# PSUM banks of the expert stage handed out in the order they come back, and the scatter sums and the next gather placed later

## The chip, the cores and the metric

The kernel runs on one core of a Trainium2 chip. The metric is the device time of one execution in microseconds, as the median of the runs shown. One execution was also taken by the hardware profiler; its trace is what the rows below come from. The engines are named as the profile names them: PE (matmul; PEld is its weight load), DVE (vector), ACT (scalar), POOL and SP (the queue that issues the weight loads).

## The reference, cut to what matters

The program is a two-layer transformer block followed by a second block. What the change touches is the mixture of experts: 256 tokens, 8 experts, two of them for each token.

```
for e in range(8):
    y = (silu(h @ w_gate[e]) * (h @ w_up[e])) @ w_down[e]     # 1024 -> 3584 -> 1024
    out = out + gates[..., e:e+1] * y
```

All weights are 4-byte floats: three matrices of 1024 x 3584 for each expert, some 352 MB in all for this stage, which takes about half of the time.

## The kernel before, in words

**Units.** The expert stage reads its weights in units of 1 MB (a tile of 128 x 2048). An expert has 42 of them, and the program passes them in one fixed order written out in Python. The expert's 3584 columns are cut into four slices f (1024, 1024, 1024, 512). For a slice come its gate units, its up units, and then the down units of the slice before it (`STEPS`, `wide`, `down`). A slice of 1024 has 4 + 4 + 4 units, so the first slice of a later expert has 4 gate units, 4 up units and the 2 last down units of the expert before it; slices 1 and 2 have twelve units each, and slice 3 has eight. Below, f0 to f3 are these slices and "unit 5 of f1" counts from the slice's first gate unit.

**One unit.** Each weight tile is split into two parts so that fp32 products can be made from faster matmuls. ACT casts it to `w_hi` (line 86), DVE subtracts to get `w_lo` (line 87), PE multiplies. There are three pairs of `w_hi`/`w_lo`, so ACT's cast for unit n + 3 waits until PE has finished unit n. `Weights.ahead` issues the split of unit n + 2 before the other work of unit n, so on ACT and DVE, which work in program order, everything placed in unit n stands behind the split of unit n + 2. SP issues the load into a freed raw buffer (line 148).

**Two kinds of experts.** Only the tokens of an expert are computed, gathered into 128 columns. If an expert has at most 64 tokens, both parts of the tokens fit side by side into one stationary operand and a unit takes 8 matmuls of 512 columns (line 1306, `few_`); otherwise it takes 12 (lines 1297, 1299, 1301, `many`). PE chooses at run time. By the lines that run, experts 0, 1, 2, 4 and 7 are of the small kind here and 3, 5 and 6 of the large kind.

**Work beside the units.** `later(n, do)` puts a piece of work n units ahead, and `later(n, do, 1)` puts it behind the matmuls of that unit. Each 512-column result of a gate or an up lies in a PSUM bank: one unit after the result is complete ACT copies it out (line 1374), one unit after that PE turns it into another bank (lines 1359, 1363), and one unit after that ACT (silu, line 1383) or DVE (product, line 1391) reads it. When an expert's last down unit is done, its two accumulators are split (lines 443, 444), and `scatter` sends the result back to the token order: for each half c of the columns and each half t of the tokens two matmuls (line 1439) into a bank, and one unit later DVE adds the bank, times the gate, into `x` (line 1447). The two sums of c = 0 are made after unit 3 of the next expert's f1, those of c = 1 after unit 4. `gather` prepares the following expert: DVE builds a selection matrix (lines 1185 and 1187), PE multiplies it twice into a bank (line 1323), each result is split by ACT and DVE (lines 443, 444), and a transpose follows (lines 1331, 1333). It starts at unit 7 of f1, its matmuls come after units 8, 10 and 12.

**Banks.** Two of the eight PSUM banks hold the accumulators `acc`. The other six form the pool `psum`, whose tiles the framework hands out with the waits that the reuse of a tile's bank needs. `wide` asks for its two banks before its first unit.

Of the kernel before, what the change touches and what calls it, by code (L numbers as in the profile page):

```python
# [203 lines left out]
def lm_kernel(ctx: ExitStack, tc: tile.TileContext, g, out: bass.AP, start=None, stop=None):  # L204
# [244 lines left out]
    class Prep:  # L449
# [67 lines left out]
        def spread(self, psum, tag="ps"):  # L517

            ps = psum.tile([128, 512], F32, name=tag)
            nc.tensor.matmul(ps[:, 0:T], ones, flat(self.diag), start=True, stop=True)  # L520
            R = work.tile([128, T], F32, name="R", bufs=2)
            nc.scalar.copy(R, ps[:, 0:T])  # L522
            self.R = R
            return R[:, None, :].to_broadcast([128, 2, T])

# [604 lines left out]
    def moe(prep, stack):  # L1130
# [83 lines left out]
        psum = pool_of(stack, "moe_ps", 6, True)  # L1214
# [34 lines left out]
        def experts(W, r0, picked=None, late=None):  # L1249
# [61 lines left out]
            def gather(e):  # L1311
                P = picked if picked is not None and e == 0 else pick(e, r0)
                X[e] = parted(xp, 8, "xe", bufs=2)
                if not r0:
                    more[e] = nc.values_load(counts[0:1, e:e + 1], engines=[mybir.EngineType.PE], min_val=0, max_val=T)
                yield
                for half_ in range(2):
                    hs = slice(half_ * 4, half_ * 4 + 4)
                    ps = psum.tile([128, 4, CAP], F32, name="ps")
# [6 lines left out]
                    split_psum(sl(X[e][1:], S_, hs), ps)  # L1326
                    yield
                PT[e] = p.tile([128, T], F32R, name="PT", bufs=2)
                ps = psum.tile([128, 512], F32, name="ps")
# [3 lines left out]
                nc.scalar.copy(PT[e], ps[:, 0:T])  # L1333

# [5 lines left out]
            def wide(name, e, f, after={}):  # L1340

                nh, n = SIZES[f] // 512, 2048 // SIZES[f]
                ps = [psum.tile([128, 512], F32, name="ps") for _ in range(nh)]
                for u in range(8 // n):
                    step(name, lambda w: products(
                        e, [(ps[c], sl(X[e], S_, u * n + k), sl(w, S_, k, half(c))) for k in range(n) for c in range(nh)],
                        lambda i: u == 0 and i < nh, lambda i: u == 8 // n - 1 and i >= (n - 1) * nh))
                    if u in after:
                        after[u]()
                return ps  # L1350

            def turn(e, s):

                ps = psum.tile([128, 4, 128], F32, name="ps")
# [11 lines left out]
                return ps  # L1366

            def turn_later(e, c, ps, use):
# [3 lines left out]
                def copy():  # L1372
                    box["s"] = xp.tile([128, 512], F32, name="s", bufs=2)
                    nc.scalar.copy(box["s"], ps)  # L1374

                later(1 + c, copy)
                later(2 + c, lambda: box.update(ps=turn(e, box["s"])), 1)
                later(3 + c, lambda: use(box["ps"]))
# [19 lines left out]
            def down(e, f):  # L1398
# [9 lines left out]
                if not last or e < LAST:  # L1408
# [8 lines left out]
                    if last:  # L1417
                        for c in range(2):
                            later(1 + c, lambda a=sl(y, S_, half(c)), b=acc[c]: split_psum(a, b))
                            scatter(e, c, 3 + c)  # L1420
# [13 lines left out]
            def scatter(e, c, n=None):  # L1434

                def multiply(t):
                    ps = psum.tile([128, 512], F32, name="ps")
# [7 lines left out]
                def add(t, ps):  # L1445
                    xs = x[:, t, half(c)]
                    nc.vector.scalar_tensor_tensor(xs, ps, gates[:, t, e:e + 1], xs, op0=OP.mult, op1=OP.add)

                for t in range(2):
                    if n is None:  # L1450
                        multiply(t)
                    else:
                        later(n, lambda t=t: multiply(t), 1)
# [9 lines left out]
            for s in STEPS + [None]:  # L1463
# [5 lines left out]
                if f == 1 and e < LAST:  # L1469
                    gather_later(STEPS[STEPS.index((e, NS - 1)) + 1][0], 7)  # L1470
# [819 lines left out]
```

## Time and profile before

| what | value |
|---|---|
| runs shown (3) | median 1785.62 us, 1784.87 to 1785.79 us |
| profiled execution, its own time | 1785.14 us |
| its span in the trace | 1783.4 us |
| mean granted PE clock | 0.985 |
| expert stage in the trace | from about 434 us (unit 0 split) to about 1390 us |
| weight loads of the stage | 336 of 1 MB |

In the windows below, each stretch of the expert stage runs from DVE's split of a slice's first unit to that of the next slice's first unit, so it holds one slice's split work. "Busy" of PE is the time in which matmuls are in flight, which isn't the same as PE at its peak. A timeline row gives the start, the duration (of several merged instructions together), and in brackets how long the engine had been idle and what ended that.

### The profile page before, as it was taken

How to read it: one execution, taken by the hardware profiler on the slowest of the kernel's cores; microseconds unless marked ns; L12 is line 12 of the kernel's file. 1: busy time of each engine (PE TensorE's matmuls, PEld its weight loads, DVE VectorE, ACT ScalarE, POOL GpSimd, SP SyncE). 2: the span in 40 equal slices, each digit the busy share in tenths (PEclk: the TensorE clock that was granted, in tenths of full speed). 3: DMA queues.
4: the chain of work that ended last, by engine and by line, in shares of the span. 5: the costliest groups of instructions: out<-in, count | busy, mean ns of one | idle time of the engine just before them, and what ended most of it. 6: DMA issues, size and time to landing. Idle time of an engine off the chain costs nothing. (4 is left out here: it accounts for less than half of the span.)

```text
span 1783.4 us, 24452 instructions
## 1 busy us (share of the span) xinstructions
PE 1707.3 (96%) x9381; PEld 1438.6 (81%) x9381; DVE 1428.9 (80%) x1365; ACT 1157.1 (65%) x1103; POOL 57.5 (3%) x104
## 2 busy tenths in 40 slices
PE   8999999999999898999999999999999899999999
PEld 7879999998777776778877778888777678789998
DVE  4666655775999999898899998887899788579776
ACT  4544444464888788887787876776879544546553
POOL 1001000120000000000000000000001100000000
PEclk9999999999999999999999999999999899999999
DMA  7546555448999999999899998998997443236552
GB/s 253 165 130 203 189 189 187 159 146 308 375 373 412 353 399 410 367 412 347 314 390 353 401 396 308 349 352 314 345 387 285 148 153 128 77 112 200 188 189 71
DMA packets 176043, 483.18 MB, mean 271 GB/s; under 512 B 8183, under 2 KB 71793, under 8 KB 161554
## 3 DMA queue, kind: packets, MB, share of 16 engines
q1 hardware_dynamic: 173762, 476.09, 72.8%
q0 software_dynamic: 2128, 4.91, 1.0%
q8 instruction: 113, 1.85, 0.4%
q14 instruction: 40, 0.33, 0.1%
HBM read 479.92 MB, written 1.05 MB: 270 GB/s over the span
## 5 line engine op out<-in xcount | busy, mean ns | idle before, releaser
L87 DVE TENSOR_TENSOR w_lo<-raw,w_hi 128x2048 fp32r<-128x2048 f32 x219 | 499.8, 2290 | 135.7 <-ACT w_hi L86 135.5
L86 ACT CAST w_hi<-raw 128x2048 fp32r<-128x2048 f32 x219 | 417.1, 1909 | 225.3 <-issue 87.2
L411 PE MATMUL ps<-hT_hi,w_hi 128*128 128x256 f32 x704 | 199.6, 284 | 0.1
L412 PE MATMUL ps<-hT_lo,w_hi 128*128 128x256 f32 x704 | 199.5, 283 | 0.1
L413 PE MATMUL ps<-hT_hi,w_lo 128*128 128x256 f32 x704 | 199.3, 283 | 0.0
L87 DVE TENSOR_TENSOR w_lo<-ahead,w_hi 128x2048 fp32r<-128x2048 f32 x78 | 177.0, 2287 | 20.7 <-ACT w_hi L86 20.6
L87 DVE TENSOR_TENSOR w_lo<-spare,w_hi 128x2048 fp32r<-128x2048 f32 x75 | 170.2, 2287 | 21.3 <-ACT w_hi L86 21.2
L1306 PE MATMUL ps<-w_lo,xe 128*128 128x512 f32 x560 | 162.6, 413 | 19.6 <-DVE w_lo L87 18.3
L1306 PE MATMUL ps<-w_hi,xe 128*128 128x512 f32 x560 | 162.6, 412 | 17.6 <-ACT s L1374 8.4
L86 ACT CAST w_hi<-ahead 128x2048 fp32r<-128x2048 f32 x78 | 147.6, 1906 | 33.9 <-PE ps L1299 12.3
L86 ACT CAST w_hi<-spare 128x2048 fp32r<-128x2048 f32 x75 | 141.9, 1907 | 29.8 <-PE ps L1299 8.7
L1306 PEld LDWEIGHTS ps<-w_lo,xe 128*128 128x128 f32 x560 | 103.3, 192 | 64.3 <-DVE w_lo L87 43.2
L1306 PEld LDWEIGHTS ps<-w_hi,xe 128*128 128x128 f32 x560 | 104.2, 194 | 42.5 <-ACT s L1374 10.1
L412 PEld LDWEIGHTS ps<-hT_lo,w_hi 128*128 128x128 f32 x704 | 134.6, 191 | 1.5 <-DVE hT_lo L444 0.8
L411 PEld LDWEIGHTS ps<-hT_hi,w_hi 128*128 128x128 f32 x704 | 134.6, 191 | 1.0 <-ACT R L522 0.2
L413 PEld LDWEIGHTS ps<-hT_hi,w_lo 128*128 128x128 f32 x704 | 134.6, 191 | 0.3 <-DVE w_lo L87 0.3
L87 DVE TENSOR_TENSOR w_lo<-hT_lo,w_hi 128x2048 fp32r<-128x2048 f32 (+1 forms) x53 | 118.9, 2245 | 14.5 <-ACT w_hi L86 14.3
L86 ACT CAST w_hi<-hT_lo 128x2048 fp32r<-128x2048 f32 (+1 forms) x53 | 99.5, 1880 | 22.3 <-PE acc L1299 7.7
L1297 PE MATMUL ps<-w_hi,xe 128*128 128x512 f32 x336 | 95.3, 405 | 2.0 <-ACT s L1374 2.0
L1301 PE MATMUL ps<-w_lo,xe 128*128 128x512 f32 x336 | 92.4, 397 | 0.0
L1299 PE MATMUL ps<-w_hi,xe 128*128 128x512 f32 x336 | 92.3, 396 | 0.0
L1306 PE MATMUL acc<-w_lo,hp 128*128 128x512 f32 x280 | 90.2, 405 | 1.9 <-DVE w_lo L87 1.0
(480 smaller groups left out, 3393.1 us busy)
## 6 DMA issues: line engine op xcount, KB each, us to landing
raw<-in_moe_w_up_dram SPq DMA_DIRECT2D x38, 1024.0 KB, 7.6
raw<-in_moe_w_gate_dram SPq DMA_DIRECT2D x34, 1024.0 KB, 8.0
raw<-in_moe_w_down_dram SPq DMA_DIRECT2D x33, 1024.0 KB, 7.1
ahead<-in_moe_w_up_dram SPq DMA_DIRECT2D x28, 1024.0 KB, 8.0
spare<-in_moe_w_down_dram SPq DMA_DIRECT2D x27, 1024.0 KB, 7.1
ahead<-in_moe_w_down_dram SPq DMA_DIRECT2D x26, 1024.0 KB, 6.7
spare<-in_moe_w_gate_dram SPq DMA_DIRECT2D x24, 1024.0 KB, 7.6
spare<-in_moe_w_up_dram SPq DMA_DIRECT2D x24, 1024.0 KB, 7.4
```

Of the source, the lines that this page charges most:

```text
L86: self.nc.scalar.copy(hi[at], src[at])
L87: self.nc.vector.tensor_sub(lo[at], src[at], hi.bitcast(F32)[at])
L411: nc.tensor.matmul(o, ah, bh, start=first, stop=False, **kw)
L412: nc.tensor.matmul(o, ah, bl, start=False, stop=False, **kw)
L413: nc.tensor.matmul(o, al, bh, start=False, stop=last, **kw)
L1297: nc.tensor.matmul(o, a, b, start=first(n), stop=False)
L1299: nc.tensor.matmul(o, a, b, start=False, stop=False)
L1301: nc.tensor.matmul(o, a, b, start=False, stop=last(n))
L1306: nc.tensor.matmul(o, a[:, HALF:HALF + CAP], b[i], start=not i and first(n), stop=i == 1 and last(n))
```

## The change

There are three parts. First, the pool's six rotating tiles become six lasting tiles held by a small class `Banks`: `take` hands out the one that was given back first, and each user gives its bank back (`back`) right behind the instruction that reads it last. `wide` takes its banks in its first unit, not before it. Second, the four scatter sums are made one at a time: after units 3 and 5 of f1 for c = 0, after units 8 and 10 for c = 1. Third, the next expert's gather starts at unit 11 of f1 where it started at unit 7, so its matmuls come after unit 12 of f1 and after units 2 and 4 of f2. The instructions themselves stay the same, and so do the weights' order and loads.

```
--- before.py
+++ after.py
@@ -522,6 +522,28 @@
             nc.scalar.copy(R, ps[:, 0:T])
             self.R = R
             return R[:, None, :].to_broadcast([128, 2, T])
+
+    class Banks:
+
+
+        def __init__(self, pool, n):
+            self.free = [pool.tile([128, 512], F32, name=f"ps{i}") for i in range(n)]
+
+        def take(self):
+            return self.free.pop(0)
+
+        def back(self, t):
+            assert all(t is not a for a in self.free)
+            self.free.append(t)
+
+        def tile(self, shape, dt, name=None):
+
+            t = self.take()
+            self.back(t)
+            return t if len(shape) == 2 else in_four(t)
+
+    def in_four(ps):
+        return ps[:, 0:512].rearrange("p (a b) -> p a b", a=4)
 
     def spread_row(ps, t, c):
         nc.tensor.matmul(ps, ones[0:1], t[0:1, half(c)], start=True, stop=True)
@@ -1211,7 +1233,7 @@
 
         prep.stack.close()
         work.stack.close()
-        psum = pool_of(stack, "moe_ps", 6, True)
+        psum = Banks(pool_of(stack, "moe_ps", 1, True), 6)
         accp = pool_of(stack, "moe_acc", 2, True)
         xp = pool_of(stack, "moe_x")
         spare = stack.enter_context(ExitStack())
@@ -1316,7 +1338,8 @@
                 yield
                 for half_ in range(2):
                     hs = slice(half_ * 4, half_ * 4 + 4)
-                    ps = psum.tile([128, 4, CAP], F32, name="ps")
+                    bank = psum.take()
+                    ps = in_four(bank)
                     for i in range(4):
                         k = half_ * 4 + i
                         for t in range(2):
@@ -1324,13 +1347,15 @@
                                              start=t == 0, stop=t == 1)
                     yield
                     split_psum(sl(X[e][1:], S_, hs), ps)
+                    psum.back(bank)
                     yield
                 PT[e] = p.tile([128, T], F32R, name="PT", bufs=2)
-                ps = psum.tile([128, 512], F32, name="ps")
+                ps = psum.take()
                 for t in range(2):
                     nc.tensor.transpose(ps[:, tok(t)], P[:, t], ident)
                 yield
                 nc.scalar.copy(PT[e], ps[:, 0:T])
+                psum.back(ps)
 
             def gather_later(e, n):
                 g = gather(e)
@@ -1340,18 +1365,25 @@
             def wide(name, e, f, after={}):
 
                 nh, n = SIZES[f] // 512, 2048 // SIZES[f]
-                ps = [psum.tile([128, 512], F32, name="ps") for _ in range(nh)]
+                ps = []
+
+                def mult(w):
+                    if not u:
+                        ps.extend(psum.take() for _ in range(nh))
+                    products(
+                        e, [(ps[c], sl(X[e], S_, u * n + k), sl(w, S_, k, half(c))) for k in range(n) for c in range(nh)],
+                        lambda i: u == 0 and i < nh, lambda i: u == 8 // n - 1 and i >= (n - 1) * nh)
+
                 for u in range(8 // n):
-                    step(name, lambda w: products(
-                        e, [(ps[c], sl(X[e], S_, u * n + k), sl(w, S_, k, half(c))) for k in range(n) for c in range(nh)],
-                        lambda i: u == 0 and i < nh, lambda i: u == 8 // n - 1 and i >= (n - 1) * nh))
+                    step(name, mult)
                     if u in after:
                         after[u]()
                 return ps
 
             def turn(e, s):
 
-                ps = psum.tile([128, 4, 128], F32, name="ps")
+                bank = psum.take()
+                ps = in_four(bank)
                 at = [s[:, i * 256 + j:(i + 1) * 256:2] for i in range(2) for j in range(2)]
 
                 def many():
@@ -1363,7 +1395,7 @@
                         nc.tensor.matmul(ps[:, i], at[i], fold, start=True, stop=True)
 
                 either(e, many, few_)
-                return ps
+                return bank
 
             def turn_later(e, c, ps, use):
 
@@ -1372,10 +1404,15 @@
                 def copy():
                     box["s"] = xp.tile([128, 512], F32, name="s", bufs=2)
                     nc.scalar.copy(box["s"], ps)
+                    psum.back(ps)
+
+                def used():
+                    use(in_four(box["ps"]))
+                    psum.back(box["ps"])
 
                 later(1 + c, copy)
                 later(2 + c, lambda: box.update(ps=turn(e, box["s"])), 1)
-                later(3 + c, lambda: use(box["ps"]))
+                later(3 + c, used)
 
             def gate(e, f, ps):
                 sg = sgs[e, f] = xp.tile([128, 8, 128], F32, name="sg")
@@ -1417,7 +1454,7 @@
                     if last:
                         for c in range(2):
                             later(1 + c, lambda a=sl(y, S_, half(c)), b=acc[c]: split_psum(a, b))
-                            scatter(e, c, 3 + c)
+                            scatter(e, c, (3 + 5 * c, 5 + 5 * c))
                     return
                 ws = W.get(*["md"] * n)
                 for c in range(2):
@@ -1434,7 +1471,7 @@
             def scatter(e, c, n=None):
 
                 def multiply(t):
-                    ps = psum.tile([128, 512], F32, name="ps")
+                    ps = psum.take()
                     for i in range(2):
                         nc.tensor.matmul(ps, PT[e][:, tok(t)], ys[e][i][:, half(c)], start=i == 0, stop=i == 1)
                     if n is None:
@@ -1445,12 +1482,13 @@
                 def add(t, ps):
                     xs = x[:, t, half(c)]
                     nc.vector.scalar_tensor_tensor(xs, ps, gates[:, t, e:e + 1], xs, op0=OP.mult, op1=OP.add)
+                    psum.back(ps)
 
                 for t in range(2):
                     if n is None:
                         multiply(t)
                     else:
-                        later(n, lambda t=t: multiply(t), 1)
+                        later(n[t], lambda t=t: multiply(t), 1)
 
             to_come = gather(0)
             take(to_come, 3)
@@ -1467,7 +1505,7 @@
                     break
                 e, f = s
                 if f == 1 and e < LAST:
-                    gather_later(STEPS[STEPS.index((e, NS - 1)) + 1][0], 7)
+                    gather_later(STEPS[STEPS.index((e, NS - 1)) + 1][0], 11)
                 gate(e, f, wide("mg", e, f, {} if prev else {8 * SIZES[f] // 4096 - 1: begun}))
                 up(e, f, wide("mu", e, f))
                 if prev:
```

## Rows read from the trace of the kernel before

**Rows 1.** The page's first part: busy time, share of the span, instructions of each engine.

```profile
PE 1707.3 (96%) x9381; PEld 1438.6 (81%) x9381; DVE 1428.9 (80%) x1365; ACT 1157.1 (65%) x1103; POOL 57.5 (3%) x104
```

**Rows 2.** Windows: stretch, length, busy us by engine (count), granted clock, DMA share, GB/s.

```profile
463.30:496.10 32.80, 30.47 (x169) 25.50 (x167) 31.73 (x28) 28.65 (x27) 0.00 (x0) 1.00 1.01 393
496.10:529.10 33.00, 31.24 (x153) 24.50 (x152) 29.96 (x19) 26.99 (x24) 0.00 (x0) 1.00 0.97 368
574.20:611.00 36.80, 31.87 (x157) 25.80 (x156) 34.56 (x27) 29.08 (x27) 0.00 (x0) 0.91 1.00 388
611.00:643.90 32.90, 31.13 (x152) 24.40 (x151) 29.86 (x18) 26.89 (x23) 0.00 (x0) 1.00 0.93 344
643.90:663.90 20.00, 18.30 (x84) 13.73 (x83) 20.00 (x12) 17.41 (x14) 0.00 (x0) 1.00 1.02 411
687.60:723.50 35.90, 31.87 (x163) 26.53 (x162) 34.30 (x27) 28.16 (x25) 0.00 (x0) 0.95 1.02 406
803.00:842.00 39.00, 38.33 (x188) 31.49 (x187) 34.65 (x27) 29.31 (x25) 0.00 (x0) 1.00 0.93 352
928.80:965.60 36.80, 33.77 (x172) 28.06 (x171) 34.50 (x27) 28.78 (x25) 0.00 (x0) 0.95 1.00 386
1302.20:1339.40 37.20, 33.83 (x159) 27.18 (x158) 33.17 (x24) 28.13 (x24) 0.00 (x0) 0.95 0.97 375
1339.40:1368.20 28.80, 26.63 (x123) 20.59 (x123) 28.80 (x16) 26.25 (x21) 1.54 (x4) 1.00 0.93 356
```

**Rows 3.** Waits, 420 to 1330 us: total us, times, longest.

```profile
PE ps L1306 <- ACT s L1374: 8.4, 4, 3.2
...
PE ps L1306 <- DVE x L1447: 6.2, 4, 1.6
...
PE ps L1297 <- ACT s L1374: 2.0, 3, 0.7
```

**Rows 4.** Timeline of PE in the change from expert 0 to 1.

```profile
585.60 1.12 PE L1439 MATMUL ps<-xe,PT 128*128 128x512 f32 x4
589.90 0.79 PE L1306 MATMUL ps<-w_hi,xe 128*128 128x512 f32 x1 [3.19 <-ACT s L1374]
592.03 1.65 PE L1306 MATMUL ps<-w_hi,xe 128*128 128x512 f32 x3 [1.33 <-DVE x L1447]
...
595.18 1.80 PE L1306 MATMUL ps<-w_hi,xe 128*128 128x512 f32 x4
...
603.35 1.95 PE L1323 MATMUL ps<-P,hT_hi 128*128 128x128 f32 x16
```

**Rows 5.** Timeline of ACT in the same stretch.

```profile
589.27 0.58 ACT L1374 COPY s<-ps 128x512 f32<-128x512 f32 x1
593.71 1.90 ACT L86 CAST w_hi<-ahead 128x2048 fp32r<-128x2048 f32 x1 [3.86 <-PE ps L1306]
...
597.02 1.90 ACT L86 CAST w_hi<-ahead 128x2048 fp32r<-128x2048 f32 x1 [0.93 <-PE ps L1306]
```

**Rows 6.** Windows: the ten microseconds around that wait.

```profile
586.00:596.00 10.00, 5.48 (x13) 3.67 (x13) 10.00 (x9) 6.14 (x5) 0.00 (x0) 0.70 1.03 408
```

**Rows 7.** Timeline of DVE in the same stretch.

```profile
585.62 2.28 DVE L87 TENSOR_TENSOR w_lo<-hT_hi,w_hi 128x2048 fp32r<-128x2048 f32 x1
...
591.23 1.41 DVE L1447 SCALAR_TENSOR_TENSOR x<-ps,gates,x 128x512 f32<-128x512 f32 x2
...
601.17 0.48 DVE L1185 TENSOR_SCALAR P<-iota,slot 128x128 f32<-128x128 f32 x2
601.68 0.35 DVE L1187 SCALAR_TENSOR_TENSOR P<-P,few 128x128 f32<-128x128 f32 x1
...
606.76 0.68 DVE L444 TENSOR_TENSOR xe<-ps,xe 128x512 fp32r<-128x512 f32 x1
608.68 2.29 DVE L87 TENSOR_TENSOR w_lo<-raw,w_hi 128x2048 fp32r<-128x2048 f32 x1 [1.24 <-ACT w_hi L86]
610.96 2.29 DVE L87 TENSOR_TENSOR w_lo<-spare,w_hi 128x2048 fp32r<-128x2048 f32 x1
```

More of the change, by code (lines that the diff above doesn't have):

```diff
@@ L524, in spread, with __init__, take, back @@
             return R[:, None, :].to_broadcast([128, 2, T])
+    class Banks:
+        def __init__(self, pool, n):
+            self.free = [pool.tile([128, 512], F32, name=f"ps{i}") for i in range(n)]
+        def take(self):
+            return self.free.pop(0)
+        def back(self, t):
+            assert all(t is not a for a in self.free)
+            self.free.append(t)
+        def tile(self, shape, dt, name=None):
+            t = self.take()
+            self.back(t)
+            return t if len(shape) == 2 else in_four(t)
+    def in_four(ps):
+        return ps[:, 0:512].rearrange("p (a b) -> p a b", a=4)
     def spread_row(ps, t, c):
@@ L1213, in moe @@
         work.stack.close()
-        psum = pool_of(stack, "moe_ps", 6, True)
+        psum = Banks(pool_of(stack, "moe_ps", 1, True), 6)
         accp = pool_of(stack, "moe_acc", 2, True)
@@ L1318, in gather @@
                     hs = slice(half_ * 4, half_ * 4 + 4)
-                    ps = psum.tile([128, 4, CAP], F32, name="ps")
+                    bank = psum.take()
+                    ps = in_four(bank)
                     for i in range(4):
@@ L1326, in gather @@
                     split_psum(sl(X[e][1:], S_, hs), ps)
+                    psum.back(bank)
                     yield
                 PT[e] = p.tile([128, T], F32R, name="PT", bufs=2)
-                ps = psum.tile([128, 512], F32, name="ps")
+                ps = psum.take()
                 for t in range(2):
@@ L1333, in gather @@
                 nc.scalar.copy(PT[e], ps[:, 0:T])
+                psum.back(ps)
             def gather_later(e, n):
@@ L1342, in wide, with mult @@
                 nh, n = SIZES[f] // 512, 2048 // SIZES[f]
-                ps = [psum.tile([128, 512], F32, name="ps") for _ in range(nh)]
+                ps = []
+                def mult(w):
+                    if not u:
+                        ps.extend(psum.take() for _ in range(nh))
+                    products(
+                        e, [(ps[c], sl(X[e], S_, u * n + k), sl(w, S_, k, half(c))) for k in range(n) for c in range(nh)],
+                        lambda i: u == 0 and i < nh, lambda i: u == 8 // n - 1 and i >= (n - 1) * nh)
                 for u in range(8 // n):
-                    step(name, lambda w: products(
-                        e, [(ps[c], sl(X[e], S_, u * n + k), sl(w, S_, k, half(c))) for k in range(n) for c in range(nh)],
-                        lambda i: u == 0 and i < nh, lambda i: u == 8 // n - 1 and i >= (n - 1) * nh))
+                    step(name, mult)
                     if u in after:
@@ L1352, in turn @@
             def turn(e, s):
-                ps = psum.tile([128, 4, 128], F32, name="ps")
+                bank = psum.take()
+                ps = in_four(bank)
                 at = [s[:, i * 256 + j:(i + 1) * 256:2] for i in range(2) for j in range(2)]
@@ L1365, in turn @@
                 either(e, many, few_)
-                return ps
+                return bank
             def turn_later(e, c, ps, use):
@@ L1374, in copy, with used @@
                     nc.scalar.copy(box["s"], ps)
+                    psum.back(ps)
+                def used():
+                    use(in_four(box["ps"]))
+                    psum.back(box["ps"])
                 later(1 + c, copy)
                 later(2 + c, lambda: box.update(ps=turn(e, box["s"])), 1)
-                later(3 + c, lambda: use(box["ps"]))
+                later(3 + c, used)
             def gate(e, f, ps):
@@ L1436, in multiply @@
                 def multiply(t):
-                    ps = psum.tile([128, 512], F32, name="ps")
+                    ps = psum.take()
                     for i in range(2):
@@ L1447, in add @@
                     nc.vector.scalar_tensor_tensor(xs, ps, gates[:, t, e:e + 1], xs, op0=OP.mult, op1=OP.add)
+                    psum.back(ps)
                 for t in range(2):
```

6 lines of the change are left out of this document (3 added, 3 removed).

## The prediction

> **What bounds the kernel now.** I read the page's busy line first [rows 1]: PE 96%, DVE 80%, ACT 65%. That is an average over stages, so I cut the expert stage into its slices by windows [rows 2]. The two kinds of experts have different limits. In a large expert PE is the bound: in f1 of expert 3 it is busy 38.33 of 39.0 us. In a small expert it is DVE: f3 of expert 1 has DVE busy 20.00 of 20.0 us, and the twelve units of f1 keep it busy for 34.56 of 36.8.
>
> The reader should compare f1 with f2 in these windows. A plain slice (f2 of expert 1) takes 32.9 us. f1 of expert 0, which holds a gather but no scatter, takes 32.8, so a gather is nearly free there. f1 of experts 1, 2 and 4, with scatter and gather, takes 36.8, 35.9 and 36.8, and f1 of expert 7, with a scatter alone, 37.2. So the small experts' f1 is long where a scatter is in it. The table of waits shows something that goes with it [rows 3]: PE waited for banks that ACT had still to copy (8.4 us in 4 waits) and for banks that DVE had still to add (6.2 us in 4), once each in these four slices; in the three large experts 2.0 us in 3 waits.
>
> The timeline of one such place shows the mechanism. After the four scatter sums PE has all six banks out: four sums and two gate results. The first up unit (unit 5) needs two, and PE stands 3.19 us for the copy of a gate result and then 1.33 us for the first sum to be added [rows 4]. DVE loses nothing at that moment: it is busy 10.00 of 10 us around it [rows 6]. The loss comes behind it. PE's delay holds back the release of `w_hi`, so ACT stands 3.86 us before the split of unit 8 and 0.93 before the next [rows 5], and DVE, once its backlog is gone, waits for ACT: 1.24 us at unit 12 [rows 7] and smaller pieces before. The granted clock drops too, to 0.70 of full on average in that stretch [rows 6]: part of it ran at 1.2 GHz in place of 2.4.
>
> **The change part by part.** No instruction is added or removed, and no load moves in SP's queue; POOL has nothing here.
>
> *Banks in the order of return.* Walking through the program with both other parts in place, every bank that is taken was last read at least two units before. The closest case is the turn after unit 6, which takes the bank of the first sum, added in unit 4. In the order of DVE this add stands right behind the split of unit 6, which PE needs for unit 6 itself, so the turn could wait some tenths; I set it at 0. The large experts' three waits go, and since PE is the bound there, they are worth their full 2.0 us [rows 3].
>
> *Scatter sums one by one.* What does a small expert's f1 take without the waits? From below DVE limits it. In the window of f1, which ends with the split of unit 13, DVE no longer has the last add (it moves to unit 11, behind that split; half of 1.41 us, so 0.70), the selection matrix (0.48 + 0.35 = 0.83) and one split of the gather (0.68) [rows 7]: together 2.21 us. Expert 1 has 34.56 - 2.21 = 32.35 left of 36.8, a saving of up to 4.45; expert 2, 34.30 - 2.21 = 32.09 of 35.9, 3.81; expert 4, 34.50 - 2.21 = 32.29 of 36.8, 4.51; expert 7, with only the add moved, 33.17 - 0.70 = 32.47 of 37.2, 4.73 [rows 2]. Sum 17.5 us, the upper end.
>
> Can ACT keep DVE that busy? I replay expert 1. Unit 5 is then bound by its `w_lo`, ready at 585.62 + 2.28 = 587.90 [rows 7]; four more matmuls, at 1.1 us for four [rows 4], end it at about 589.0. ACT is free after its copy at 589.27 + 0.58 = 589.85 [rows 5] and can begin the split of unit 8 there, where it began at 593.71: 3.9 us earlier. DVE reaches unit 8 later than that, so it doesn't wait. Followed on in the same way, ACT stays ahead through unit 13, which DVE begins at about 606.5 in place of 610.96 [rows 7]: 4.5 us, the full saving. The replay leaves out what signals between engines take, so I take back 0.5 us for each of the four slices: 2.0.
>
> *The later gather.* What leaves f1 comes back in f2, and its matmuls (1.95 us each group of 16 [rows 4]) now stand behind unit 12 and behind gate units 2 and 4 of f2. From above, f2 grows by the whole vector work: 2.21 for each of experts 1, 2 and 4, 0.70 for expert 7, and for expert 0, whose gather moves too, 0.83 + 0.68 = 1.51; sum 8.8 us. From below it grows by nothing: a plain f2 has 32.9 - 29.86 = 3.04 us of idle DVE, and the pair of expert 0 (gather 32.8, none 33.0) [rows 2] shows a gather inside a slice at no cost. In expert 7, f2 has no idle time (DVE 28.80 of 28.8), so its 0.70 counts in full. I take 1.0 for each of the three, 0 for expert 0 and 0.7 for expert 7, nearer to the pair because it is the same work in the same kind of slice: 3.7 us. In the large experts PE's sum is the same wherever the gather stands: 0. The gather's result is first used in the next expert, some twenty units later, so its lateness costs nothing.
>
> Could DMA become the bound? In f3 it moves 411 GB/s at a share of 1.02, in f1 388 [rows 2]. Twelve units in 32.9 us are about 382 GB/s, so there is room over a whole expert, but little in f3; I set it at 0.
>
> **Sum:** 17.5 + 2.0 - 2.0 - 3.7 = 13.8 us less. The profiled execution took 1785.14 us, so 1771.3; the median of the runs shown is 0.48 above it, so **1771.8 us** in their terms. The 1.7 us around the span stay. Ends: everything saved and nothing given back, 19.5 us, gives 1766.1; with f2 at its full price and DVE idle in f1 as much as in expert 2 before (1.6 us in each of four, 6.4), 17.5 + 2.0 - 8.8 - 6.4 = 4.3 us, gives 1781.3.
>
> **The rivals.**
> *The wait was hidden (no gain but in the large experts).* DVE is busy 10.00 of 10 us around the wait [rows 6]; if its later idle time belongs to the loop of three buffers and not to the lead that was lost, f1 and f2 together stay as they are. Only the 2.0 us go: 1783.6, within the bound of no change. Against it: f1 of expert 0 has the gather and no such length. The Trainium skill ("TensorE: Matmul & The Clock Gate", the section on HAM oscillation) has a kernel of which it says "Adding PSUM double-buffering gave no further gain"; by that the small experts would gain 0. The trace speaks against it here only through the ACT waits behind the stall. Chance 0.06.
>
> *The gather pays in full.* Gather matmuls between gate units delay PE, hence ACT, hence DVE, and f2 grows by all 2.21 us and some idle. That is 17.5 + 2.0 - 8.8 - 4 for four slices at 1 us of idle each = 6.7 us less: 1778.9. For it: a plain slice already shows DVE idle, so the loop is tight. Chance 0.13.
>
> *Slower: the later gather breaks the loop of f2.* If each of the gather's two large groups on PE delays ACT's split by its full 1.95 us and the loop has no slack, f2 of experts 0, 1, 2 and 4 grows by 4 x 3.9 = 15.6 us, the vector work of 8.8 beside it uncovered: 17.5 + 2.0 - 2.0 - 15.6 - 8.8 = 6.9 us more, 1792.5. The point from which it decides: f2 of these experts above 32.9 + 4.4 = 37.3 us on average. Against it: f1 of expert 0 holds the same groups at 32.8 [rows 2]. Chance 0.06.
>
> *The change doesn't do what it says.* Lasting tiles might carry waits that rotating ones don't, for instance across the branches that write them; then PE's waits stay and only their names change, about 1785.6. The users and the branches are the same as before. Chance 0.03.
>
> **How the numbers follow.** The forecast has 0.72. A measurement of this kernel can tell about 0.2%, 3.6 us, from no change, so faster means below 1782.0. Faster: 0.72 + 0.13 = 0.85; within: 0.06 + 0.03 = 0.09; slower: 0.06. The range runs from just under the lower end, 1765.5, over the case in which the gather pays in full, to 1779.5, and leaves out the rest.
>
> **What would show it.** Right: the bank waits on line 1306 (14.6 us) are gone or below 2 us; f1 of experts 1, 2, 4 and 7 takes 32 to 34 us, f2 up to 34; ACT's wait at unit 8 is gone; the granted clock is 1.00 through f1; the large experts lose 0.7 us each. Wrong: f1 short and f2 long by the same amount (the gather pays), f1 unchanged with PE waiting for `w_lo` where it waited for banks (hidden), or ACT waiting for loads.

## The result, and the profile after

The changed kernel takes 1765.86 us (median of 4 runs, 1764.60 to 1767.02); the kernel before took 1785.24 us beside it (median of 4, 1784.85 to 1785.79). The ratio is 0.9892, with a 95% interval of 0.9881 to 0.9904: 19.4 us faster, where 13.8 were forecast. The profiled execution took 1767.02 us, its span is 1765.2 us, 18.2 less than before, and its granted clock is 0.988 where it was 0.985.

The first part of the page of the changed kernel (busy us, share, instructions) looks like that of before [rows 1]. The count of matmuls is the same, and only 4.7 of the 18.2 us have left PE's busy time:

```profile
PE 1702.6 (96%) x9381; PEld 1432.9 (81%) x9381; DVE 1427.2 (81%) x1365; ACT 1155.8 (65%) x1103; POOL 57.4 (3%) x104
```

As before, the stage is read by slices. These are the windows of the changed kernel, with the columns of [rows 2]: f1 and f2 of expert 0, f1 and f2 of expert 1, f1 of expert 2, f1 and f2 of expert 3, f1 of expert 4, f1 and f2 of expert 7.

```profile
463.30:494.80 31.50, 29.84 (x152) 24.19 (x151) 30.61 (x24) 28.00 (x26) 0.00 (x0) 1.00 1.01 402
494.80:527.30 32.50, 31.53 (x168) 25.75 (x168) 31.04 (x22) 27.47 (x24) 0.00 (x0) 1.00 1.00 382
572.50:605.80 33.30, 30.63 (x148) 23.37 (x146) 32.25 (x21) 28.47 (x25) 0.00 (x0) 1.00 1.02 409
605.80:638.90 33.10, 30.79 (x160) 24.64 (x159) 31.64 (x23) 26.91 (x24) 0.00 (x0) 1.00 1.00 368
682.60:714.60 32.00, 30.49 (x147) 23.76 (x146) 32.00 (x22) 27.67 (x24) 0.00 (x0) 1.00 1.02 414
794.30:829.90 35.60, 35.60 (x164) 29.14 (x163) 32.54 (x21) 28.76 (x25) 0.00 (x0) 1.00 0.99 383
829.90:871.60 41.70, 41.70 (x206) 34.68 (x205) 32.26 (x23) 28.07 (x25) 0.00 (x0) 1.00 0.83 288
919.00:951.80 32.80, 32.23 (x154) 25.24 (x153) 32.14 (x22) 28.19 (x24) 0.00 (x0) 1.00 1.02 407
1286.50:1319.40 32.90, 32.31 (x155) 25.35 (x154) 32.21 (x23) 28.29 (x24) 0.00 (x0) 1.00 1.01 402
1319.40:1348.90 29.50, 27.25 (x128) 21.21 (x128) 29.50 (x19) 26.02 (x21) 1.58 (x4) 1.00 0.95 371
```

Against [rows 2], f1 of experts 1, 2, 4 and 7 went from 36.8, 35.9, 36.8 and 37.2 to 33.3, 32.0, 32.8 and 32.9 us. In expert 2 DVE is now busy for all of its 32.00 us. The granted clock is 1.00 in each of them, where it was 0.91 to 0.95. f2 grew little: from 32.9 to 33.1 in expert 1, from 28.8 to 29.5 in expert 7, and in expert 0 it even fell from 33.0 to 32.5. In expert 3, f1 went from 39.0 to 35.6 and f2 from 39.4 (the window below, from the trace of before) to 41.7: the gather moved, and 1.1 to 1.2 us of the sum are gone.

```profile
842.00:881.40 39.40, 39.40 (x183) 32.21 (x182) 30.13 (x18) 27.42 (x23) 0.00 (x0) 1.00 0.84 300
```

PE's waits of the changed kernel, in the same stretch as [rows 3] (us in total, times, longest):

```profile
PE ps L1328 <- DVE w_lo L87: 16.6, 31, 1.3
...
PE ps L1346 <- DVE P L1209: 2.3, 4, 1.3
...
PE ps L1395 <- DVE x L1484: 0.6, 4, 0.2
```

Line 1328 is what was 1306, 1319 was 1297, 1346 was 1323, 1395 was 1363, 1406 was 1374, 1476 was 1439, 1484 was 1447, and 1207 and 1209 were 1185 and 1187. The waits for a bank that ACT still copies or DVE still adds (14.6 us on line 1306) are gone but for 0.6 us at the turn. The timeline of PE shows the place of [rows 4] after the change. The first up unit (unit 5) starts its `w_hi` part without a wait at 583.88 and then waits for its own `w_lo`, as the replay had it. Two scatter matmuls follow it (one sum), not eight for four sums, and the turn behind unit 6 waits 0.15 us for the first sum's bank.

```profile
583.88 1.10 PE L1328 MATMUL ps<-w_hi,xe 128*128 128x512 f32 x4
586.24 1.20 PE L1328 MATMUL ps<-w_lo,xe 128*128 128x512 f32 x4 [1.26 <-DVE w_lo L87]
587.28 0.63 PE L1476 MATMUL ps<-xe,PT 128*128 128x512 f32 x2
...
590.40 1.18 PE L1395 MATMUL ps<-count,s 128*128 128x128 f32 x8 [0.15 <-DVE x L1484]
```

On ACT the splits of units 8 and 9, which had waited 3.86 and 0.93 us [rows 5], now start at 588.04 and 590.32 with no wait in their rows. The first is 5.67 us earlier than before, of which 1.7 were gained ahead of this slice:

```profile
588.04 1.90 ACT L86 CAST w_hi<-ahead 128x2048 fp32r<-128x2048 f32 x1
589.84 0.58 ACT L1406 COPY s<-ps 128x512 f32<-128x512 f32 x1
590.32 1.90 ACT L86 CAST w_hi<-ahead 128x2048 fp32r<-128x2048 f32 x1
```

DVE's split of unit 334, near the stage's end, starts 19.35 us earlier in the span than before (1368.87 against 1388.22); about 1.2 of it is given back behind the stage.

### The profile page after: what moved, and what is told of

It reads as the page before. It is cut to its first block, busy times and chain, and to the rows that moved or that the text cites. A ratio compares the mean times of both kernels' runs of the same rounds, so it can differ in the third digit from the quotient of the medians.

```text
span 1765.2 us, 24387 instructions
## 1 busy us (share of the span) xinstructions
PE 1702.6 (96%) x9381; PEld 1432.9 (81%) x9381; DVE 1427.2 (81%) x1365; ACT 1155.8 (65%) x1103; POOL 57.4 (3%) x104
## 5 line engine op out<-in xcount | busy, mean ns | idle before, releaser
L1328 PE MATMUL ps<-w_hi,xe 128*128 128x512 f32 x560 | 157.8, 404 | 3.0 <-DVE xe L444 3.0
L1319 PE MATMUL ps<-w_hi,xe 128*128 128x512 f32 x336 | 95.0, 404 | 0.0
L1321 PE MATMUL ps<-w_hi,xe 128*128 128x512 f32 x336 | 92.4, 397 | 0.0
```

The source lines that it names most:

```text
L1319: nc.tensor.matmul(o, a, b, start=first(n), stop=False)
L1321: nc.tensor.matmul(o, a, b, start=False, stop=False)
L1328: nc.tensor.matmul(o, a[:, HALF:HALF + CAP], b[i], start=not i and first(n), stop=i == 1 and last(n))
```

## The experiments

The theory was that of the prediction: with four sums made at once PE runs out of banks, and what that costs is ACT's lead. Its rivals were that the new order of banks alone does it, that the later gather does it, or that all three are needed. Each part was run alone and each pair together, and then what the pairs left open. In the kernels built from the kernel before, the line numbers are those of before.

| kernel | median, us | before beside it, us | ratio, 95% interval |
|---|---|---|---|
| banks alone | 1790.92 | 1784.89 | 1.0035 (1.0022 to 1.0048) |
| sums one by one alone | 1775.35 | 1784.89 | 0.9948 (0.9935 to 0.9961) |
| later gather alone | 1784.81 | 1784.89 | 1.0001 (0.9992 to 1.0009) |
| banks and sums | 1775.12 | 1784.89 | 0.9943 (0.9930 to 0.9955) |
| banks and gather | 1790.37 | 1783.68 | 1.0033 (1.0022 to 1.0044) |
| sums and gather | 1764.79 | 1783.68 | 0.9892 (0.9877 to 0.9908) |
| banks, earlier sums, old gather | 1767.17 | 1783.68 | 0.9901 (0.9886 to 0.9916) |
| all, gather from unit 13 | 1774.92 | 1783.68 | 0.9945 (0.9932 to 0.9959) |
| that, matrix in unit 11 | 1768.08 | 1784.53 | 0.9906 (0.9890 to 0.9923) |
| all, matrix in unit 9 | 1760.96 | 1784.53 | 0.9876 (0.9859 to 0.9894) |
| earlier sums, matrix in unit 5 | 1761.83 | 1784.53 | 0.9870 (0.9853 to 0.9886) |
| sums and gather, matrix in unit 9 | 1761.82 | 1785.73 | 0.9867 (0.9850 to 0.9883) |

### One part alone

**The banks alone**: the changed kernel with the old places of the sums and of the gather.

```diff
-                            scatter(e, c, (3 + 5 * c, 5 + 5 * c))
+                            scatter(e, c, (3 + c, 3 + c))
-                    gather_later(STEPS[STEPS.index((e, NS - 1)) + 1][0], 11)
+                    gather_later(STEPS[STEPS.index((e, NS - 1)) + 1][0], 7)
```

> Six lasting banks, first back first taken; the four scatter sums and the gather stay where they were (after units 3 and 4 of f1; gather from unit 7). By the order of the program the two up banks of unit 5 are then those of the first two sums, which DVE adds in unit 4, so PE waits for DVE where it waited for ACT and DVE. Theory (the lost lead of ACT): the wait at unit 5 ends at about the same time as before, so f1 of the small experts stays at 36 to 37 us and the time within 2 us of the kernel before, 1783 to 1787. Rival (the order of the banks is the gain): f1 falls to 33 and the time to about 1768 to 1772.

A miss: it was slower by 6.0 us, above the 1783 to 1787 expected. The order of return didn't remove the wait, it changed what is waited for. PE's waits of this kernel:

```profile
PE ps L1328 <- DVE x L1484: 17.3, 4, 5.4
...
PE ps L1319 <- DVE x L1484: 3.2, 3, 1.2
```

Its PE timeline between expert 0 and 1, and the window of the ten microseconds of [rows 6]:

```profile
585.17 1.12 PE L1476 MATMUL ps<-xe,PT 128*128 128x512 f32 x4
591.69 2.21 PE L1328 MATMUL ps<-w_hi,xe 128*128 128x512 f32 x4 [5.39 <-DVE x L1484]
```

```profile
586.00:596.00 10.00, 4.61 (x13) 3.27 (x12) 9.85 (x10) 5.48 (x5) 0.00 (x0) 0.66 1.02 404
```

Before, PE waited 3.19 us for ACT's copy and then 1.33 for a sum [rows 4]. Here it waits 5.39 us in one piece for a sum, and the total is 20.5 us where [rows 3] have 16.6. As long as all six banks are out, the order in which they are handed out can only choose whose return ends the wait, and DVE's adds come later than ACT's copy. In expert 1 the wait still ends 17.9 us behind the slice's start (17.8 before), and f1 keeps its 36.7 us, as the theory had it. The loss lies in the other experts: f1 grew by 0.4 us in expert 2, by 1.5 and 1.4 in experts 4 and 7, where its granted clock is 0.91 against the 0.95 of [rows 2], and by 0.5 to 0.7 in each large expert.

**The sums one by one alone**: the kernel before with four sums in four units.

```diff
-                            scatter(e, c, 3 + c)
+                            scatter(e, c, (3 + 5 * c, 5 + 5 * c))
-                        later(n, lambda t=t: multiply(t), 1)
+                        later(n[t], lambda t=t: multiply(t), 1)
```

> Only the scatter sums are spread over units 3, 5, 8 and 10, with the rotating pool and the gather from unit 7 as before. Theory: with two sums fewer outstanding at unit 5 PE's long wait there goes if the pool hands out a bank that was already read; then f1 of the small experts falls to 33 to 35 us and the time to 1768 to 1776. Where the rotation hands out the bank of a result that is copied in the same unit, a wait of 1 to 3 us comes back at another unit and half of the gain goes, 1776 to 1782. Rival (vector work moved from f1 to f2 is the gain): one add of 0.7 us moves in each of seven experts, 1780 or more.

The time came within what was expected, about half of the gain, but not in the expected way. All waits for banks were gone, with the old rotating banks. Yet f1 of experts 1 and 2 rose, to 37.4 and 37.1 us, where 33 to 35 were expected, while their f2 fell by 1.2 and 2.8. Only f1 of expert 7, which has no gather, fell to the 32.9 that it has in the whole change. Experts 1, 2 and 4 gained 0.5, 1.6 and 1.7 us in all, where the whole change gives them 3.2, 3.7 and 3.8; the large experts gained 0.9 to 1.1, nearly as much as in it. The waits of ACT in this kernel show a new one in each of the six slices that hold sums and a gather, and PE waits 6.0 us for the selection matrix (1.7 before, in one wait):

```profile
ACT xe L443 <- PE ps L1439: 43.6, 6, 7.4
```

```profile
PE ps L1323 <- DVE P L1187: 6.0, 4, 1.7
```

**The later gather alone**: the kernel before with one number changed.

```diff
-                    gather_later(STEPS[STEPS.index((e, NS - 1)) + 1][0], 7)
+                    gather_later(STEPS[STEPS.index((e, NS - 1)) + 1][0], 11)
```

> Only the gather goes from unit 7 to unit 11 of f1, with the rotating pool and the scatter as before. Theory: PE's wait at unit 5 stays (about 14 us in all on line 1306), so f1 shrinks by no more than the 1.5 us of vector work that leaves it, f2 grows by part of it, and the time is 1782 to 1786. Rival (the gather's place is the gain): f1 33 to 34 us and 1770 to 1776.

No change in the time, as expected: PE's waits for banks stayed (8.4 and 6.3 us). By slices it is a sum of two things. f1 and f2 of expert 0, which has no sums, take 1.7 us less, as in the whole change; f1 of experts 1, 2, 4 and 7 grew by 0.5 to 1.3 us, where it was expected to shrink or stay. Why it grew stays open.

### Two parts

**Banks and sums**: the changed kernel with the gather from unit 7.

```diff
-                    gather_later(STEPS[STEPS.index((e, NS - 1)) + 1][0], 11)
+                    gather_later(STEPS[STEPS.index((e, NS - 1)) + 1][0], 7)
```

> Lasting banks and spread scatter sums, the gather from unit 7 as before. Theory: the waits for banks at unit 5 are gone, ACT keeps its lead, and most of the gain is there: f1 of the small experts 33 to 35 us with the gather's vector work still in it, f2 at 32.9, time 1766 to 1771. Rival (the later gather carries it): 1778 or more.

A miss: 1775.12, the time of the sums alone, slice by slice the same to 0.05 us, but for the first slice of the stage (0.13). What is missing against the whole change is therefore the gather's place. By slices it is 1.8 us in expert 0, which has no sums, and 6.9 in experts 1, 2 and 4 together. The timeline of ACT and PE in expert 2 shows why the early gather costs these three:

```profile
711.25 1.91 ACT L86 CAST w_hi<-spare 128x2048 fp32r<-128x2048 f32 x1 [0.33 <-PE ps L1328]
720.30 0.59 ACT L443 CAST xe<-ps 128x512 fp32r<-128x512 f32 x1 [7.15 <-PE ps L1476]
720.78 0.59 ACT L1406 COPY s<-ps 128x512 f32<-128x512 f32 x1
721.26 1.91 ACT L86 CAST w_hi<-spare 128x2048 fp32r<-128x2048 f32 x1
```

```profile
713.99 2.05 PE L1346 MATMUL ps<-P,hT_hi 128*128 128x128 f32 x16 [1.39 <-DVE P L1209]
...
719.63 0.63 PE L1476 MATMUL ps<-xe,PT 128*128 128x512 f32 x2
```

The gather's first result is ready on PE at about 716, yet ACT's split of it (line 443) starts at 720.30, behind the last sum (719.63). The code says what ties them. There are two `xe` buffers. The result y of an expert is written into that expert's own `xe` (line 1406 of before), the sums read it there in the next expert's f1, and the gather in that f1 writes the same buffer for the expert after. The gather from unit 7 splits its first half in unit 9, and the last sum now stands behind unit 10. ACT works in order: it stands for 7.15 us, and a copy and a weight split that don't need the gather stand behind it. The Trainium skill ("PSUM — Partial Sum Buffer", section "Engine vs sequencer instructions") says that the queues of ScalarE and VectorE are strictly first in, first out; this trace agrees, the two rows behind the stall start 0.48 us apart as soon as it ends.

**Banks and gather**: the changed kernel with the old places of the sums.

```diff
-                            scatter(e, c, (3 + 5 * c, 5 + 5 * c))
+                            scatter(e, c, (3 + c, 3 + c))
```

> Lasting banks and the later gather, with the sums after units 3 and 4 as before. Theory: PE waits at unit 5 for the sums' adds on DVE as with the banks alone (17 us there), and the gather's place changes nothing by itself: 1788 to 1793, slower than the kernel before. Rival (the gather's place is worth its 10 us in any company): 1778 to 1783.

Slower by 6.7 us, as expected: it keeps the 17.3 us of the banks alone.

**Sums and gather, without lasting banks**: the kernel before with the edits of the two single parts.

```diff
-                            scatter(e, c, 3 + c)
+                            scatter(e, c, (3 + 5 * c, 5 + 5 * c))
-                        later(n, lambda t=t: multiply(t), 1)
+                        later(n[t], lambda t=t: multiply(t), 1)
-                    gather_later(STEPS[STEPS.index((e, NS - 1)) + 1][0], 7)
+                    gather_later(STEPS[STEPS.index((e, NS - 1)) + 1][0], 11)
```

> The spread sums and the later gather, with the rotating pool as before; only the lasting banks are left out. In the runs so far the kernel with the spread sums took the same time with either pool (1775.35 and 1775.12). Theory now (the spread sums end the bank waits in either pool, and the later gather takes away a wait of ACT for the last sum, since the gathered tokens of the next expert go into the buffer from which the sums read): 1765 to 1768, no different from the whole change. Rival (the banks' order of return is needed): 1770 or more, with PE waits on banks of over 4 us in all.

1764.79 us, ratio 0.9892, the ratio of the whole change. Every slice of the eight experts agrees with it to 0.02 us, but for the first slice of the stage. So the lasting banks add nothing that can be measured here: once the sums come one by one, rotating banks have no wait either.

### What the order of sums and gather costs

**Earlier sums, old gather**: the banks, the sums after units 3, 5, 6 and 8, so that the last sum stands before the first split of a gather that still begins in unit 7.

```diff
-                            scatter(e, c, (3 + 5 * c, 5 + 5 * c))
+                            scatter(e, c, (3 + 3 * c, 5 + 3 * c))
-                    gather_later(STEPS[STEPS.index((e, NS - 1)) + 1][0], 11)
+                    gather_later(STEPS[STEPS.index((e, NS - 1)) + 1][0], 7)
```

> Lasting banks, the gather from unit 7 as before, and the sums spread less far, after units 3, 5, 6 and 8, so that the last is made before the gather's first split in unit 9. Theory (ACT's wait for the last sum is what the early gather costs beside sums that end at unit 10): the 43 us of ACT's waits on line 443 for line 1476 fall under 8, and the time to 1766 to 1771. Rival (gather and sums crowd the same units on PE and DVE, whatever the buffer): 1773 to 1777.

1767.17, as the theory of the shared buffer has it: the gather was not moved at all, and ACT's waits for the sums (43.5 us in 6 with banks and sums) are gone. Against banks and sums, experts 1, 2 and 4 are 2.6 us shorter each, 7.8 together, and expert 0 is unchanged. What matters in these experts is the order of the two, not the gather's lateness.

**The gather from unit 13**: the whole change with one number changed.

```diff
-                    gather_later(STEPS[STEPS.index((e, NS - 1)) + 1][0], 11)
+                    gather_later(STEPS[STEPS.index((e, NS - 1)) + 1][0], 13)
```

> The whole change with the gather from unit 13 in place of 11, so that all of it stands in f2 of a slice, behind the last add. Theory: nothing waits for the gather before the next expert, and f1 loses the selection matrix more: 1764 to 1768, within 2 us of the whole change. Rival (the later, the better): 1763 or less.

A miss, some 9 us slower than the whole change. The row to read is one of PE's waits:

```profile
PE ps L1346 <- DVE P L1209: 9.4, 4, 2.4
```

The timelines of PE and DVE in expert 1 of this kernel:

```profile
618.22 2.46 PE L1346 MATMUL ps<-P,hT_hi 128*128 128x128 f32 x16 [2.38 <-DVE P L1209]
620.34 2.05 PE L1328 MATMUL ps<-w_hi,xe 128*128 128x512 f32 x4
```

```profile
615.11 2.28 DVE L87 TENSOR_TENSOR w_lo<-spare,w_hi 128x2048 fp32r<-128x2048 f32 x1
617.31 0.47 DVE L1207 TENSOR_SCALAR P<-iota,slot 128x128 f32<-128x128 f32 x2
617.82 0.35 DVE L1209 SCALAR_TENSOR_TENSOR P<-P,few 128x128 f32<-128x128 f32 x1
```

DVE builds the selection matrix one unit before PE multiplies by it, and behind the split of a unit that comes two later. PE reaches the gather first and stands, and the unit behind it is late with it: f2 of experts 1, 2 and 4 took 36.0, 34.5 and 37.2 us, where the whole change has 33.1 in each.

**The same gather with its matrix two units earlier**: on the kernel just shown, only the building of the matrix moves, to unit 11.

```diff
-                    later(n + i, lambda: next(g, None), i in (1, 3, 5))
+                    later(n + i if i else n - 2, lambda: next(g, None), i in (1, 3, 5))
```

> The whole change with the gather's matmuls from unit 14 (gather from 13) as in all_gather13, but its selection matrix built in unit 11, two units ahead of where that run had it. Theory (all_gather13 lost its 9 us because DVE builds the matrix behind the split of unit 15 and PE, which wants it after unit 14, stands 2.2 to 2.4 us for it in each of four slices, and ACT after PE): PE's waits on the matrix, 9.4 us there, fall under 1, and the time to 1764 to 1769. Rival (matmuls of a gather among gate units cost it, matrix or not): 1773 to 1776.

1768.08: PE's waits for the matrix are gone, and with them most of the 9 us.

**The whole change with the matrix in unit 9**: the same edit on the changed kernel, which still had 2.3 us of that wait.

```diff
-                    later(n + i, lambda: next(g, None), i in (1, 3, 5))
+                    later(n + i if i else n - 2, lambda: next(g, None), i in (1, 3, 5))
```

> The whole change with the selection matrix built in unit 9 in place of 11, all else as in it. Theory: PE's remaining waits on the matrix (2.3 us) go, and some of ACT's behind them; 1761 to 1765. Rival (DVE is full there, so the matrix costs the same wherever it stands): 1765 to 1768.

1760.96 us, just under what was expected. The windows of f1 and f2 of expert 1 in this kernel:

```profile
571.00:603.80 32.80, 30.29 (x146) 23.60 (x147) 32.76 (x25) 29.07 (x24) 0.00 (x0) 1.00 1.02 408
603.80:636.20 32.40, 30.93 (x163) 25.03 (x162) 30.97 (x20) 26.40 (x24) 0.00 (x0) 1.00 0.99 380
```

Together 65.2 us where the whole change has 66.4. Experts 1, 2 and 4 are 1.1, 1.7 and 1.7 us shorter, expert 0 is 0.2 shorter in f1 and f2, and the large experts are unchanged: 4.7 us in this trace.

**Earlier sums with the matrix in unit 5**: the same edit on the kernel of the earlier sums.

```diff
-                    later(n + i, lambda: next(g, None), i in (1, 3, 5))
+                    later(n + i if i else n - 2, lambda: next(g, None), i in (1, 3, 5))
```

> early_sums (sums after units 3, 5, 6 and 8, gather from 7) with the selection matrix built in unit 5. Theory: PE's 5.6 us of waits on the matrix go; the small experts 0 and 1 gain a us or more each, 1762 to 1766. Rival (DVE is full in f1, so the earlier matrix only delays the adds): 1766 to 1769.

1761.83 us, again just under. Experts 1, 2 and 4 are 1.2 us shorter each and expert 0 is 1.8 shorter. The windows of f1 and f2 of expert 0 and of f2 of expert 2 in this kernel (32.9, 32.9 and 30.6 us with the earlier sums alone):

```profile
463.61:496.17 32.56, 31.88 (x178) 26.80 (x177) 31.81 (x29) 28.55 (x27) 0.00 (x0) 1.00 1.01 397
496.17:527.61 31.44, 29.70 (x143) 23.09 (x142) 29.78 (x19) 26.86 (x23) 0.00 (x0) 1.00 1.01 378
715.85:745.27 29.42, 27.89 (x134) 22.03 (x133) 29.42 (x19) 26.68 (x22) 0.00 (x0) 1.00 1.02 391
```

**Sums and gather with the matrix in unit 9, without lasting banks**: the same edit on the kernel of sums and gather.

```diff
-                    later(n + i, lambda: next(g, None), i in (1, 3, 5))
+                    later(n + i if i else n - 2, lambda: next(g, None), i in (1, 3, 5))
```

> The kernel before with its rotating bank tiles, the scatter sums one by one, the gather from unit 11, and the selection matrix already built in unit 9. If the lasting banks contribute nothing once the sums are spread, and if building the matrix early is worth what the trace of it with lasting banks shows (1.1 to 1.7 us in each of experts 1, 2 and 4), this gives 1759 to 1763 us, ratio 0.986 to 0.988, with no wait for the matrix. If the gain of the early matrix was scatter between executions, it gives 1764 to 1766, ratio 0.989 to 0.990. If the lasting banks matter together with the early matrix, it gives more than 1767.

1761.82 us, ratio 0.9867, inside what was expected. In each slice but the first of the stage its trace agrees with that of the whole change with the early matrix to 0.03 us. The three kernels with an early matrix have ratios of 0.9867 to 0.9876, their three fellows without it 0.9892 to 0.9901. The intervals of a pair overlap or touch, but the three pairs and the slices point the same way, so these versions beat both kernels; by how much over the changed one, some 3 to 6 us, is not settled more closely.

## Why the prediction was right, and where it was wrong

The forecast was 1771.8 us, in a range of 1765.5 to 1779.5; 1765.86 lies just inside its lower end. The direction and the mechanism held: PE's delay at unit 5 costs ACT's lead, and without it f1 is as short as DVE allows. The sizes of three small terms and one attribution did not hold, and the errors of the small terms all point the same way, which is why the time lies at the lower end.

- **f1 of the small experts: right.** 17.5 less 2.0 for friction, 15.5 us, was forecast. Measured are 36.8 - 33.3 = 3.5, 35.9 - 32.0 = 3.9, 36.8 - 32.8 = 4.0 and 37.2 - 32.9 = 4.3, together 15.7. The sum fits better than its parts, and that is luck: with 0.5 taken off each saving, expert 1 was set at 3.95 (the replay had its full 4.5) and expert 2 at 3.31, and the two misses cancel. The walk that took DVE's moved work out of the window (32.09 us left in expert 2) met the 32.00 of the trace.
- **The give-back in f2: sized too large.** 3.7 us were set, 1.0 for each of experts 1, 2 and 4 and 0.7 for expert 7. Measured are 0.2 in each of the three and 0.7: 1.3 us. DVE's idle time of 3.04 us in a plain slice covered the gather almost wholly; where it could not (expert 7, DVE busy throughout), the price was the full 0.7. But those 3.04 us don't belong to a plain slice as such. With the earlier sums and the matrix in unit 5, f2 of expert 2 is just as plain and takes 29.42 us with DVE busy throughout: the idle time was a delay carried over from f1.
- **Expert 0: set at 0, gained 1.7 us.** Its f1 fell by 1.3 and its f2 by 0.4. The step that failed is the reading of the pair in [rows 2], gather 32.8 and none 33.0, as "nearly free": two different slices were compared. The same slice without its gather takes 31.5, so the gather had cost 1.3 there. The trace of before has PE waiting 1.7 us for the selection matrix in f1 and f2 of expert 0, the changed one 0.4 (first row before, second after):

```profile
PE ps L1323 <- DVE P L1187: 1.7, 1, 1.7
PE ps L1346 <- DVE P L1209: 0.4, 1, 0.4
```

  That wait is the cause, and the gather as such is not. With the earlier sums, building the matrix two units earlier, and nothing else, takes f1 and f2 of expert 0 from 65.8 to 64.0 us together, with the gather still in f1; the changed kernel has 64.1. Most of that gain shows in f2, so the wait in f1 had lengthened f2 as well, and "none 33.0" was no slice without a gather's cost. The forecast had moved the matrix as DVE work only and not asked who waits for it.
- **The large experts: 2.0 us set, 3.2 measured** (1.15, 1.15 and 0.93 by slices). The forecast took the bare wait, 0.67 us each. The timeline of PE in expert 3 before shows the rest:

```profile
818.64 1.08 PE L1439 MATMUL ps<-xe,PT 128*128 128x512 f32 x4
820.39 1.42 PE L1297 MATMUL ps<-w_hi,xe 128*128 128x512 f32 x4 [0.67 <-ACT s L1374]
821.64 1.10 PE L1299 MATMUL ps<-w_hi,xe 128*128 128x512 f32 x4
```

  Elsewhere in that timeline groups of four such matmuls start 0.91 to 0.94 us apart (1.02 behind a turn). Here the group behind the scatter starts 820.39 - 818.64 = 1.75 after it, 0.81 more, and the next one 1.25 after that, 0.31 more. So an idle time of 0.67 us cost PE 1.12. By the starts of single matmuls (0.23 apart otherwise) the three waits cost 1.14, 1.13 and 0.92 in experts 3, 5 and 6, with an idle time of 0.66 to 0.67 in each: to 0.02 us what each of them gained.
- **What the parts do: wrong.** The forecast credited the order of return with the end of the large experts' waits. The pair without it equals the whole change, the sums alone end these waits, and the banks alone cost 6.0 us. The walk through the banks was made "with both other parts in place", so it could not tell which part removed the waits; with rotating banks the trace shows none either. It also did not ask what the later gather is for. The shared buffer stands nowhere in it, though it made the third part a condition of the second. Its order is worth 7 to 8 us: of what lies between 1775.12 and 1765.86, 6.9 us are in experts 1, 2 and 4, and the earlier sums gave the same experts 7.8.
- **The turn after unit 6: 0 set, 0.6 us measured** in four waits, as the row of waits shows. It made no visible difference: the pair with rotating banks doesn't have this wait and takes the same time.

The three small terms and f1 add up: 0.2 + 2.4 + 1.7 + 1.2 = 5.5 us more than the 13.8. That makes 19.3 us; the first slice of the stage took 0.35 more, but the stage began 0.34 earlier (DVE's split of unit 0 starts at 423.78 where it started at 424.12; the 434 in the table of before is wrong), so it is also what unit 334 gained. With about 1.2 given back behind the stage, it is the 18.2 by which the span is shorter, but for rounding.

**The rivals.** The hidden wait (1783.6) fell with f1's 15.7 us. The sentence of the Trainium skill that "Adding PSUM double-buffering gave no further gain" ("TensorE: Matmul & The Clock Gate", section on HAM oscillation) is about more buffers in another kernel, and no run here added a bank. Here PE stood for banks, and spreading the sums, so that it never does, was worth 9.5 us alone, while a new order of the same six banks cost 6.0. How much of the wait's cost was the lower granted clock no run separates; a full clock alone doesn't make f1 short, for with the sums alone it is 1.00 in f1 of expert 1 and the slice takes 37.4 us. That the gather pays in full (1778.9) fell with f2 at 33.1. The later gather that breaks f2's loop (1792.5) was to decide at an f2 above 37.3 us on average; it is 33.0 over experts 0, 1, 2 and 4. Two units later it would have come partly true (36.0, 34.5 and 37.2), by PE's wait for the matrix and not by ACT's split. That the change doesn't do what it says fell with the waits.

The signs named for "right" all came: bank waits below 2 us, f1 at 32.0 to 33.3, f2 up to 33.1, no wait of ACT at unit 8, a clock of 1.00 through f1. The 0.7 us of each large expert were 0.9 to 1.2.

## What to carry to other kernels

When a pool runs dry, look first at who takes many buffers at once; spreading the takers removed every long wait for a bank here, and handing out the same buffers in another order only changed which reader ended the wait, and made it longer. Before work is moved later, list who writes the buffer that it reads: an engine that works in order turns one early writer into a stall of everything behind it. Here it was nearly as good a cure to bring the readers (the sums) ahead of the writer (the gather) as to move the writer behind them. When a term is set at "free", compare the same stretch with and without the work, not two neighbouring stretches, since a delay in the first can lengthen the second, and count who waits for its small preparations.

## What the runs showed that was not expected

- An idle time of PE of 0.67 us cost it 1.12 us by the starts of its matmuls, at a granted clock of 1.00: the first group behind the wait took 1.25 us to the next start where 0.91 to 0.94 is usual (1.02 behind a turn).
- A longer wait shows in the clock as well: with the banks alone PE stood 5.39 us, the ten microseconds around it have a granted clock of 0.66 (0.70 before [rows 6], with waits of 3.19 and 1.33), and the group behind it took 2.21 us where 1.09 to 1.18 are usual. So part of that stretch ran at 1.2 GHz in place of 2.4.
- Within the stage slices repeat to 0.05 us or less between kernels of like code, but the very first slice does not: f0 of expert 0 took between 37.6 and 40.8 us in kernels that have the same work there. It should be taken out before slices of two traces are added up; what sets it stays open.
